# A decoder layer on one core: 46 products of the tile of ones ahead of TensorE's first real product

## The chip, the core and the metric

The kernel runs on one core of one Trainium2 chip. Its time is the device time of one launch in microseconds (us). A core has five engines, each with an instruction queue of its own that is worked through in order: TensorE (PE) for matrix products, VectorE (DVE), ScalarE (ACT), GpSimd (POOL) and SyncE (SP). SP issues all the DMA transfers of this kernel. An engine waits at an instruction until the semaphores that it needs have come, and everything behind that instruction on the same engine waits too.

## The reference

One layer of a decoder, in float32, for a prompt of 1024 tokens and 8 single-token samples that share the weights (1032 columns in all):

```python
z = x @ w_in                                   # 1024 -> 7680 columns, for all branches and gates
xr, yr, q, k, v, xq, g = jnp.split(z, SPLIT_IDX, axis=-1)
a_out = rg_lru(causal_conv(xr)) * gelu(yr)     # branch A: recurrence
s_out = sliding_window_attention(q, k, v)      # branch B: window 128, 16 heads
c_out = mem_attn(xq, mem_k, mem_v)             # branch C: 256 memory tokens, 4 heads
merged = sum(sigmoid(g_n + b_n) * (br_n @ w_branch[n]) for n in range(3))
h = layer_norm(ALPHA * x + merged @ w_out)
y = layer_norm(ALPHA * h + (silu(h @ w_gate) * (h @ w_up)) @ w_down)
```

The state of the recurrence, the last keys and values and the memory keys and values are outputs too.

## The kernel before, in words

Activations lie transposed: channels on the 128 partitions, the 1032 tokens along the free dimension. A float32 product is made of three products of the type `fp32r`: each operand is split into a high part (a cast on ACT, line L80) and a low part (a subtraction on DVE, L81), and high x high, high x low and low x high are added up in PSUM. So each tile that TensorE reads needs first a DMA, then a cast on ACT, then a subtraction on DVE.

The first stage, `project`, computes `x @ w_in` in 30 **units** of two row tiles each. Unit 0 (`begin`) is computed straight: four **quarters** of 258 columns, each with 48 products (2 halves of the channels, 2 row tiles, 4 blocks of 128 channels, 3 products each; lines L211 to L213, PSUM tile `u`, operands `th`/`tl` for x and `thw`/`tlw` for the weights). Its operands come from the first transfers: weights `ur<-win` and quarters of x, `x<-xQ`, both on SP's queue.

From unit 1 on a unit is computed with seven products of half the size in place of eight (Strassen's scheme, `fast_step`, lines L293 to L295): seven **steps** i = 0 to 6, each with 24 products of 128x258, first 12 for one half of the columns (p = 0) and then 12 for the other (p = 1). Step i needs the weights `u_ih` (ACT) and `u_il` (DVE); some of them are sums of blocks, `us`, made on DVE (L278). It needs also sums of quarters of x, made once for all units on DVE (L218, names `x`), and their casts and subtractions (`th`, `tl`). The results gather in PSUM tiles: `ub` takes the steps 0, 2, 4 and 6 one upon another, `ud` the steps 1 and 5, `uc` step 3. Between step 0 and step 2 ACT copies `ub` away (`p1s`, L318), and step 2 may not add to `ub` before that copy; in the same way `u2s` stands between the steps 2 and 4, and `zb<-ub` on DVE (L322) between the steps 4 and 6. PSUM has three `mm` buffers for `ub`, two `t` for `ud` and `u`, two `s` for `uc`, and one `o` for small things.

Beside the units run **side jobs** that other branches need. Two of them matter here. `dec_mem` (L791 on) is the memory attention of the eight samples for the first head: the query columns of unit 0 are transposed on TensorE (`drt`, L787), copied by ACT (`drow_c`, L788), written to DRAM (`dcq<-drow_c`, L789), read back broadcast to all partitions (`dcq<-dcq`, L800), and multiplied on DVE with the memory keys (`dcj`, L806). `lru` is the recurrence: DVE makes the convolution `xc` out of `za` of unit 1 (L728, L729), ACT and DVE split it (`xch`, `xcl`), and TensorE multiplies it with the gate blocks (`g`, L114 to L116, from `mm3`).

The order on each engine isn't written out by hand. The source hands all instructions to a scheduler at build time, with their dependences; it places them by priority and by times that it estimates for itself, engine by engine, and that order is then fixed in the program. `issue_after` ties a few groups behind a given instruction. An instruction that is added in one place can thus move others.

`self.ones` is a constant tile of 128x128 with 1/1024 in each element, set by DVE at the very start (L145) and used much later by the layer norms.

Of the kernel before, what the change touches and what calls it, by code (L numbers as in the profile page):

```python
# [18 lines left out]
P = 128  # L19
# [19 lines left out]
HT = T // 2  # L39
QN = T // 4  # L40
QS = 264
UNITS = (
    ("xq", 0), ("lru", 0), ("gate", 0), ("xq", 1), ("lru", 1), ("gate", 1), ("xq", 2), ("lru", 2), ("gate", 2),
    ("xq", 3), ("lru", 3), ("gate", 3), ("k", 0), ("lru", 4), ("v", 0), ("q", 0), ("lru", 5), ("gate", 4),
# [15 lines left out]
class Builder:  # L60
# [75 lines left out]
    def setup(self):  # L136
# [9 lines left out]
        self.shift = self.cst.tile([P, P], F32R, name="shift")  # L146
        nc.vector.memset(self.shift.bitcast(F32), -1.0 / (256 * MIX))

    def load_consts(self):
        nc, io = self.nc, self.io  # L150
        nc.sync.dma_start(self.vec, io["vec"])
        nc.sync.dma_start(self.ident, io["cst"][:, 0:P])
# [11 lines left out]
    def begin(self, rows, finish, load_next, next_quarter):  # L164


        nc, io, h = self.nc, self.io, D // 2
        place = lambda i: (self.tpe if i in (0, 1, 2, 3) else self.tpl, f"c{i}")

        def pair(name, i):  # L170
            pool, tag = place(i)
            return tuple(pool.tile([P, 4, QS], F32R, tag=tag, name=f"t{e}{name}", bufs=4) for e in "hl")

        x, hl, ts, w, ps = {}, {}, [[None] * 7, [None] * 7], [[None] * 2, [None] * 2], {}
        cols = lambda th, p: slice(HT * th + QN * p, HT * th + QN * (p + 1))

        def weight(j, e):
            raw = self.half_raw(io["win"][rows[j]][:, e * h:(e + 1) * h], h, f"ur0_{j}{e}")
            if e == 0:
                w[j] = [None, None, pair(f"w{j}", 4)]  # L180
            flat = [a.rearrange("p k n -> p (k n)")[:, e * h:(e + 1) * h] for a in w[j][2]]
            w[j][e] = flat
            return lambda: self.split(*flat, raw)

        def keep(name, i, src, sign=1.0):
            tiles = pair(name, i)
            hi, lo = (a[:, :, :QN] for a in tiles)
            src = src.rearrange("p (k n) -> p k n", k=4)
            if sign < 0:
                self.split_scaled(hi, lo, src, sign)  # L190
            else:
                self.split(hi, lo, src)
            return tiles

        def fetch(kh, th, p):
            x[kh, th, p] = self.x_quarter(kh, th, p)

        def block(kh, th, p):
            hl[kh, th, p] = keep(f"{kh}{th}{p}", {(0, 0): 0, (0, 1): 6, (1, 0): 3, (1, 1): 5}[kh, th], x[kh, th, p])

        def quarter(th, p, z):
            tags = ("mm", "t")
            for kh in range(2):
                xh, xl = (a[:, :, :QN] for a in hl[kh, th, p])
                for j in range(2):
                    if kh == 0:
                        ps[j] = self.bank(tags[j], f"u0{th}{p}{j}")[:, :QN]
                    wh, wl = w[j][kh]
                    for k in range(4):
                        c, first, last = slice(k * P, (k + 1) * P), kh + k == 0, kh == 1 and k == 3  # L210
                        nc.tensor.matmul(ps[j], wh[:, c], xh[:, k, :], start=first, stop=False)  # L211
                        nc.tensor.matmul(ps[j], wh[:, c], xl[:, k, :], start=False, stop=False)
                        self.last_mm = nc.tensor.matmul(ps[j], wl[:, c], xh[:, k, :], start=False, stop=last).ins  # L213
            for j in range(2):
                nc.scalar.copy(z[j][:, cols(th, p)], ps[j])

        def change(op, p, to, a, b):
            nc.vector.tensor_tensor(x[(*to, p)], x[(*a, p)], x[(*b, p)], op)  # L218
            return x[(*to, p)]

        s00 = weight(0, 0)
        fetch(0, 0, 0)
        s10, s01 = weight(1, 0), weight(0, 1)
        fetch(1, 0, 0)
        s11 = weight(1, 1)
        for th, p in ((0, 1), (1, 0), (1, 1)):
            fetch(0, th, p)
            fetch(1, th, p)
        z = self.zt("za0"), self.zt("zb0")
        s00()  # L230
        block(0, 0, 0)
        s10()
        s01()
        block(1, 0, 0)
        s11()
        quarter(0, 0, z)
        for th, p in ((0, 1), (1, 0), (1, 1)):
            block(0, th, p)
            block(1, th, p)
            quarter(th, p, z)  # L240
            if (th, p) == (1, 0):
                load_next()
                next_quarter(0)
        for p in range(2):
            ts[p][0], ts[p][3], ts[p][5] = hl[0, 0, p], hl[1, 0, p], hl[1, 1, p]
            change(ALU.subtract, p, (1, 1), (1, 1), (0, 1))
            ts[p][1] = keep(f"1_{p}", 1, change(ALU.subtract, p, (0, 1), (0, 0), (0, 1)))
        next_quarter(1)
        for p in range(2):
            ts[p][2] = keep(f"2_{p}", 2, change(ALU.add, p, (0, 0), (1, 1), (0, 0)), -1.0)  # L250
        next_quarter(2)
        next_quarter(3)
        for p in range(2):
            ts[p][4] = keep(f"4_{p}", 4, x[1, 1, p])
        for p in range(2):
            ts[p][6] = keep(f"6_{p}", 6, change(ALU.subtract, p, (1, 0), (0, 0), (1, 0)))
        views = lambda pair_: [tuple(a[:, k, :QN] for a in pair_) for k in range(4)]
        return [[views(t) for t in tp] for tp in ts], z
# [78 lines left out]
    def project(self):  # L337
# [7 lines left out]
        self.side, self.pumped = (deque(), deque()), 0  # L345
        n = len(UNITS)
        finish = [Finish(self, kind, j) for kind, j in UNITS]
        st = {}
# [1152 lines left out]
```

## Time and profile before

| | |
|---|---|
| time, median of 3 runs (range) | 1955.7 us (1953.8 to 1955.99) |
| the profiled execution | 1960.06 us, of which its span 1958.3 us |
| mean granted TensorE clock in the profile | 0.996 |
| busy share of the span: PE, DVE, ACT, POOL | 98%, 69%, 49%, 5% |
| products on PE | 14286 |
| bytes moved by DMA | 265.15 MB, mean 135 GB/s |

A row of the timeline gives the start and the length in us, the engine, the line, the operation with out<-in, the shape, how many, and in brackets the idle time before it with what ended it. Matmuls are pipelined: the length of one holds its latency, and the pace of TensorE is read from the distance between two starts. A row of the windows gives, for a stretch of time, its length and then for each engine busy us and (count), the granted TensorE clock (`PEclk`, 1.00 is full), the DMA share and GB/s. The list of waits gives who waited for whom, us in total, times, longest.

### The profile page before, as it was taken

The numbers are of one execution on the slowest core, as the hardware profiler recorded it, in microseconds if no ns is written. First come the engines' busy times: TensorE is split into PE (matmuls) and PEld (weight loads), VectorE is DVE, ScalarE is ACT, GpSimd is POOL, SyncE is SP. The second block draws the span as 40 slices with busy tenths as digits, with TensorE's granted clock in tenths as the row PEclk, the third lists the DMA queues.
The fourth block names the chain that finished last, engine by engine and source line by source line (L and its number), as shares of the span: only waits on it lengthen the run. The fifth ranks groups of instructions, "written<-read, shape, count | busy, mean of one in ns | idle before, by whom it ended". The sixth has DMA issues, their size and how long they took to land.

```text
span 1958.3 us, 37175 instructions
## 1 busy us (share of the span) xinstructions
PE 1920.2 (98%) x14286; PEld 1888.4 (96%) x14286; DVE 1345.4 (69%) x2871; ACT 960.8 (49%) x2093; POOL 99.8 (5%) x138
## 2 busy tenths in 40 slices
PE   8999999999999999999999999999999999999997
PEld 8999999999999999989999999999999999999996
DVE  8888788777766645389877457886666656734457
ACT  6556555556555545388765234644333333412214
POOL 0000012000000000011210000000000000000002
PEclk9999999999999999999999999999999999999999
DMA  5455544473233767567625242222333222523202
GB/s 212 159 189 165 181 160 164 151 239 112 84 136 124 258 221 223 152 170 213 165 71 181 88 149 77 90 66 82 114 104 98 103 87 76 185 74 124 84 1 88
DMA packets 154851, 265.15 MB, mean 135 GB/s; under 512 B 18624, under 2 KB 76816, under 8 KB 154640
## 3 DMA queue, kind: packets, MB, share of 16 engines
q1 hardware_dynamic: 154672, 262.76, 41.7%
q8 instruction: 112, 1.84, 0.4%
q14 instruction: 67, 0.55, 0.1%
HBM read 194.75 MB, written 70.03 MB: 135 GB/s over the span
## 4 chain that ended last, share of the span: by engine, by line
PE 84%; DVE 5%; ACT 5%; DMA 4%; issue 1%; SPq 0%; ACTq 0%; DVEq 0%; POOL 0%; POOLq 0%
PE ub L295 5%; PE ub L293 5%; PE ub L294 5%; PE fb L293 4%; PE fb L294 4%; PE fb L295 4%; PE d L115 3%; PE d L116 3%; PE d L114 3%; PE ud L295 2%; PE ud L294 2%; PE ud L293 2%; PE fd L293 2%; PE fd L295 2%; PE fd L294 2%; PE brs L115 2%
## 5 line engine op out<-in xcount | busy, mean ns | idle before, releaser
L582 ACT ACTIVATE bp<-bp,bst 128x257 f32<-128x257 f32 (+1 forms) x128 | 62.8, 493 | 17.6 <-DVE bst L578 17.4
L295 PE MATMUL ub<-th,u_0l 128*128 128x258 f32 x232 | 65.8, 284 | 2.1 <-DVE u_0l L81 2.1
L293 PE MATMUL ub<-th,u_0h 128*128 128x258 f32 x232 | 65.5, 282 | 1.4 <-ACT zb L1373 1.4
L1252 DVE SCALAR_TENSOR_TENSOR acc<-d,acc 128x388 f32<-128x388 f32 (+2 forms) x48 | 24.7, 514 | 61.0 <-PE d L116 61.0
L293 PE MATMUL ub<-th,u_6h 128*128 128x258 f32 x232 | 66.2, 285 | 0.3 <-DVE zb L322 0.2
L295 PE MATMUL ub<-th,u_4l 128*128 128x258 f32 x232 | 65.9, 285 | 0.3 <-DVE u_4l L81 0.3
L295 PE MATMUL ub<-th,u_2l 128*128 128x258 f32 x232 | 66.0, 285 | 0.0
L295 PE MATMUL uc<-th,u_3l 128*128 128x258 f32 x232 | 65.9, 284 | 0.0
L295 PE MATMUL ud<-th,u_1l 128*128 128x258 f32 x232 | 65.9, 284 | 0.0
L295 PE MATMUL ud<-th,u_5l 128*128 128x258 f32 x232 | 65.9, 284 | 0.0
L293 PE MATMUL uc<-th,u_3h 128*128 128x258 f32 x232 | 65.8, 283 | 0.0
L293 PE MATMUL ud<-th,u_5h 128*128 128x258 f32 x232 | 65.7, 283 | 0.0
L295 PE MATMUL ub<-th,u_6l 128*128 128x258 f32 x232 | 65.7, 283 | 0.0
L293 PE MATMUL ud<-th,u_1h 128*128 128x258 f32 x232 | 65.6, 283 | 0.0
L294 PE MATMUL ub<-tl,u_0h 128*128 128x258 f32 x232 | 65.6, 283 | 0.0
L293 PE MATMUL ub<-th,u_4h 128*128 128x258 f32 x232 | 65.6, 283 | 0.0
L293 PE MATMUL ub<-th,u_2h 128*128 128x258 f32 x232 | 65.6, 283 | 0.0
L294 PE MATMUL ub<-tl,u_2h 128*128 128x258 f32 x232 | 65.4, 282 | 0.0
L294 PE MATMUL ud<-tl,u_1h 128*128 128x258 f32 x232 | 65.4, 282 | 0.0
L294 PE MATMUL uc<-tl,u_3h 128*128 128x258 f32 x232 | 65.3, 282 | 0.0
L294 PE MATMUL ub<-tl,u_4h 128*128 128x258 f32 x232 | 65.3, 282 | 0.0
L294 PE MATMUL ud<-tl,u_5h 128*128 128x258 f32 x232 | 65.3, 282 | 0.0
(831 smaller groups left out, 8084.9 us busy)
## 6 DMA issues: line engine op xcount, KB each, us to landing
ur<-win SPq DMA_DIRECT2D x120, 256.0 KB, 2.9
urf<-wgu SPq DMA_DIRECT2D x80, 256.0 KB, 2.7
scr_f<-fo SPq DMA_DIRECT2D x36, 258.0 KB, 2.0
dck<-cmk SPq DMA_DIRECT2D x32, 256.0 KB, 3.2
dcv<-cmvT SPq DMA_DIRECT2D x32, 256.0 KB, 3.3
st<-scr_q SPq DMA_DIRECT2D x32, 256.0 KB, 4.3
S1L<-scr_f SPq DMA_DIRECT2D x14, 516.0 KB, 5.1
scr_g<-za SPq DMA_DIRECT2D x12, 516.0 KB
```

The source lines that it names most:

```text
L114: nc.tensor.matmul(ps, sh, mh, start=i == 0, stop=False)
L115: nc.tensor.matmul(ps, sh, ml, start=False, stop=False)
L116: self.last_mm = nc.tensor.matmul(ps, sl, mh, start=False, stop=closes and i == last).ins
L293: mm(sh[:, w], xh, start=opens and k == 0, stop=False)
L294: mm(sh[:, w], xl, start=False, stop=False)
L295: self.last_mm = mm(sl[:, w], xh, start=False, stop=k == 3).ins
L582: nc.scalar.activation(x, x, AF.Exp, bias=st[:, g:g + 1], scale=-1.0, accum_out=st[:, 4 + g:5 + g])
L1252: nc.vector.scalar_tensor_tensor(a, ps, MIX, a, op0=ALU.mult, op1=ALU.add)
```

## The change

A new function `keep_busy` issues 46 products of the tile of ones with itself, 128x128x128 each, into the one `o` buffer of PSUM. They add up in one accumulation group, and nobody reads the result. `begin` calls it right after the first weight and before the first quarter of x are loaded, so that they stand ahead of all other products in the source.

```diff
+WARM = 46
...
+    def keep_busy(self):
+        ps = self.bank("o", "warm")[:, :P]
+        for i in range(WARM):
+            self.nc.tensor.matmul(ps, self.ones, self.ones, start=i == 0, stop=i == WARM - 1)
...
         s00 = weight(0, 0)
+        self.keep_busy()
         fetch(0, 0, 0)
```

The lines behind these are 1 (from L42), 6 (from L150) and 7 (from L229) higher in the changed kernel; the text goes on using the numbers of the kernel before.

On TensorE the 46 products become the first instructions. They need only the memset of `ones`. Beside that the scheduler places instructions of the first 130 us or so in another order; behind that the order is the same on all engines. Three places matter. In the names `u1`, `u2` is the unit, and the last number only tells buffers apart (it is shifted by 47 in the change).

**DVE, end of unit 1.** Before, where the first low weights of unit 2 (`u2_0l`) are made:

```order
L386 SCALAR_TENSOR_TENSOR zb0_144<-zb0_144,hi_xq1_580 128x1024
L81 TENSOR_TENSOR u1_6l_602<-ur1_11_339,u1_6h_601 128x512
L806 SCALAR_TENSOR_TENSOR dcj0_0_0_597,dcs0_592<-dck0_0_595,dcq0_0_593 128x256
L320 TENSOR_TENSOR za1_605<-uc1_0_606,p1s1_0_478 128x258
L806 SCALAR_TENSOR_TENSOR dcj0_0_1_599,dcs0_592<-dck0_0_595,dcq0_0_593 128x256
L320 TENSOR_TENSOR za1_605<-uc1_1_620,p1s1_1_493 128x258
L81 TENSOR_TENSOR u2_0l_635<-ur2_00_495,u2_0h_634 128x512
```

And in the change, from the same subtraction on:

```order
L82 TENSOR_TENSOR u1_6l_649<-ur1_11_386,u1_6h_648 128x512
L327 TENSOR_TENSOR za1_652<-uc1_0_653,p1s1_0_525 128x258
L327 TENSOR_TENSOR za1_652<-uc1_1_667,p1s1_1_540 128x258
L82 TENSOR_TENSOR u2_0l_682<-ur2_00_542,u2_0h_681 128x512
L329 SCALAR_TENSOR_TENSOR zb1_685<-ub1_0_512,p5s1_0_569 128x258
...
L285 TENSOR_TENSOR us2_2_786<-us2_1_754,ur2_00_542 128x512
L813 SCALAR_TENSOR_TENSOR dcj0_0_0_644,dcs0_639<-dck0_0_642,dcq0_0_640 128x256
L689 RECIPROCAL lruc_712<-lruc_712 128x8
```

The first `dcj`, which needs the broadcast transfer `dcq`, stood four rows ahead of `u2_0l`; now it stands twelve rows behind it, after both `us` of unit 2. The rows left out are seven of the 128-partition constants of the recurrence, one `us` and one `zb`.

**TensorE, unit 2, steps 3 and 4, with the first gate product `g`.** Before:

```order
L295 MATMUL uc2_1_939<-th101_217,u2_3l_786 128x258
L114 MATMUL g0_0_0_953<-xch0_0_916,wgh0_910 128x344
L293 MATMUL ub2_0_789<-th4_0_443,u2_4h_831 128x258
...
L294 MATMUL ub2_0_789<-tl4_0_444,u2_4h_831 128x258
L115 MATMUL g0_0_0_953<-xcl0_0_917,wgh0_910 128x344
L116 MATMUL g0_0_0_953<-xch0_0_916,wgl0_911 128x344
L295 MATMUL ub2_0_789<-th4_0_443,u2_4l_832 128x258
```

In the change:

```order
L302 MATMUL uc2_1_986<-th101_264,u2_3l_833 128x258
L115 MATMUL g0_0_0_1000<-xch0_0_963,wgh0_957 128x344
L116 MATMUL g0_0_0_1000<-xcl0_0_964,wgh0_957 128x344
L117 MATMUL g0_0_0_1000<-xch0_0_963,wgl0_958 128x344
L300 MATMUL ub2_0_836<-th4_0_490,u2_4h_878 128x258
```

Eleven products of step 4 stood between the product with `xch` and the one with `xcl`; now the one with `xcl` comes at once, and all of step 4 stands behind it.

**ACT, unit 1, around the copies `p1s`.** Before:

```order
L80 CAST u1_2h_435<-us1_2_433 128x512
L80 CAST u1_3h_439<-ur1_01_335 128x512
L80 CAST th4_1_447<-x111_141 128x4x258
L318 COPY p1s1_0_478<-ub1_0_465 128x258
L318 COPY p1s1_1_493<-ub1_1_480 128x258
```

In the change:

```order
L392 ACTIVATE hi_xq0_621<-za0_190 128x1024
L81 CAST th4_1_494<-x111_188 128x4x258
L81 CAST th6_0_499<-x100_174 128x4x258
L325 COPY p1s1_0_525<-ub1_0_512 128x258
L325 COPY p1s1_1_540<-ub1_1_527 128x258
```

The cast `th6`, which needs a sum of quarters from DVE (`x100`), stood seven rows behind `p1s`; now it stands ahead of it. Further down on ACT the copy `drow_c`, which stood ahead of the casts of `u1_4h` and `u1_5h`, now stands behind both.

## The prediction

> **What bounds the kernel now.** I read the profile's page first, then the list of TensorE's waits, then the timeline where these waits lie. The page's first lines and its chain of waits:
>
> ```profile
> span 1958.3 us, 37175 instructions
> ...
> PE 84%; DVE 5%; ACT 5%; DMA 4%; issue 1%; SPq 0%; ACTq 0%; DVEq 0%; POOL 0%; POOLq 0%
> ```
>
> TensorE carries 84% of the chain that ended last. So a microsecond that TensorE loses or saves early comes through to the end, unless a later instruction waits for something else. The list of its waits over the span begins so:
>
> ```profile
> PE u L211 <- ACT th L80: 6.6, 1, 6.6
> PE ub L295 <- DVE u_0l L81: 2.1, 1, 2.1
> PE mv L446 <- ACT wmv_3h L80: 1.4, 2, 1.2
> ...
> PE ub L295 <- DVE u_4l L81: 0.3, 1, 0.3
> ```
>
> The longest is the start: 6.6 us until the first operands. The second and the fourth row belong to the end of unit 1, where the change moves instructions. Now the start in the timeline:
>
> ```profile
> 0.81 0.17 DVE L145 MEMSET ones<- 128x128 f32 x1 [0.81 <-PEq L1486]
> ...
> 6.60 1.23 DVE L81 TENSOR_TENSOR tl<-x,th 128x1032 fp32r<-128x1032 f32 x1 [1.76 <-ACT th L80]
> ...
> 7.89 0.58 PE L212 MATMUL u<-tl,thw 128*128 128x258 f32 x1 [0.17 <-DVE tl L81]
> ...
> 8.49 0.42 PE L211 MATMUL u<-th,thw 128*128 128x258 f32 x1
> ...
> 9.55 1.23 DVE L81 TENSOR_TENSOR tl<-x,th 128x1032 fp32r<-128x1032 f32 x1 [0.51 <-ACT th L80]
> ...
> 10.21 0.37 PE L213 MATMUL u<-th,tlw 128*128 128x258 f32 x1
> ...
> 10.89 0.28 PE L213 MATMUL u<-th,tlw 128*128 128x258 f32 x1
> ...
> 14.47 0.28 PE L213 MATMUL u<-th,tlw 128*128 128x258 f32 x1
> ```
>
> TensorE works without a break only from 7.89 on, when the first low part of x is there. From 8.49 to 10.21 eight products pass, 0.215 us each; from 10.89 to 14.47 thirty, 0.119 each. So TensorE starts at about half its pace and is let to the full one between 10.2 and 10.9. The row at 14.47 is the last of quarter 0.
>
> **Step 1: does the block of 46 fit into the wait?** It can start when `ones` is set, at about 1.0, and costs nothing if it is over by 7.87: 6.87/46 = 0.149 us a product. No row shows this product. The nearest:
>
> ```profile
> 710.15 1.91 PE L499 MATMUL cpt<-ident,cp 128*128 128x128 f32 x8
> 728.75 1.04 PE L499 MATMUL cpt<-ident,cp 128*128 128x128 f32 x8
> ...
> 839.83 0.23 PE L574 MATMUL bs<-ks,st 128*128 128x128 f32 x1
> 839.89 0.27 PE L575 MATMUL bs<-ks,st 128*128 128x128 f32 x1
> ```
>
> The transposes of 128x128 give the upper bound: less the latency of the last, (1.04 - 0.27)/7 = 0.11 at the full pace and (1.91 - 0.42)/7 = 0.21 at the half one. All 46 at 0.21 end at 10.8. The two `bs` products, fp32r tiles like `ones`, stand 0.06 apart, or 0.12 at half pace: all over by 6.5. I take the middle of the pair, 0.17 at half and 0.085 at full pace: with 3.6 us at half pace, as before from 6.6 to 10.2, 21 products pass, and the other 25 take 2.1 us. The block ends at about 6.7: cost nothing, hidden by the wait for x; bounds 0 and 10.8 - 7.9 = 2.9 us.
>
> [...]
>
> **Step 2: what the full pace is worth.** If the block lets the clock up, the twelve distances from 7.89 on that took 0.215 take 0.119: 12 x 0.096 = 1.15 us. The second half of quarter 0 now waits for its own low part, which is ready at 9.55 + 1.23 = 10.78 and would be asked for at about 10.7: -0.06. And one product that ran in the gap before 7.89 now stands behind it: -0.12. Quarter 1 starts 0.95 us earlier. Bounds: 0.95 and, with a block that ends at 10.8 but leaves full pace, 10.8 + 48 x 0.119 = 16.5 against 14.6, 1.9 late.
>
> [...]
>
> **Step 3: does it last to unit 1?** Rows for this and for the next steps:
>
> ```profile
> 16.16 2.38 DVE L81 TENSOR_TENSOR tl<-x,th 128x1032 fp32r<-128x1032 f32 x2 [0.87 <-ACT th L80]
> ...
> 20.98 0.69 DVE L81 TENSOR_TENSOR u_0l<-ur,u_0h 128x512 fp32r<-128x512 f32 x1 [1.30 <-ACT u_0h L80]
> ...
> 30.80 1.22 DVE L218 TENSOR_TENSOR x<-x,x 128x1032 f32<-128x1032 f32 x1
> 31.95 1.22 DVE L87 SCALAR_TENSOR_TENSOR tl<-x,th 128x1032 fp32r<-128x1032 f32 x1
> ...
> 36.58 0.68 DVE L81 TENSOR_TENSOR u_3l<-ur,u_3h 128x512 fp32r<-128x512 f32 x1
> 37.19 1.22 DVE L81 TENSOR_TENSOR tl<-x,th 128x1032 fp32r<-128x1032 f32 x1
> ...
> 47.59 0.68 DVE L81 TENSOR_TENSOR u_6l<-ur,u_6h 128x512 fp32r<-128x512 f32 x1
> ```
>
> A big DVE row costs 1.15 us (30.80 to 31.95), a weight row 0.61. Between 20.98 and 48.2, the end of `u_6l`, DVE has no gap. The change fills the gaps of 0.87 and 1.30 ahead of it (ACT's copies of `u` stand later, and one sum moves up), so I set DVE 2.2 us earlier: `u1_6l` ends at 46.0. Counting back over the twelve rows from behind `x100` to `u1_6l` (seven big ones, `x101` among them, and five weight rows): 7 x 1.15 + 5 x 0.61 = 11.1, so `x100` is ready at 34.9. Then ACT casts `th4` and `th6` (0.96 each) ahead of `p1s` (0.28): 37.1 to 37.2. Step 2, which needs that copy, would be reached at 37.57 - 0.95 = 36.6:
>
> ```profile
> 37.57 0.28 PE L293 MATMUL ub<-th,u_2h 128*128 128x258 f32 x1
> ...
> 43.56 0.28 PE L293 MATMUL ub<-th,u_4h 128*128 128x258 f32 x1
> ...
> 49.85 0.28 PE L293 MATMUL ub<-th,u_0h 128*128 128x258 f32 x1
> ```
>
> So 0.6 of the 0.95 is lost in a wait for `p1s`; some 0.3 is left.
>
> **Step 4: the wait at `u_0l`.** DVE stood at the first `dcj` until the broadcast `dcq` had landed, and `u_0l` was queued behind it:
>
> ```profile
> 50.24 0.42 DVE L806 SCALAR_TENSOR_TENSOR dcj<-dck,dcq 128x256 f32<-128x256 f32 x1 [1.98 <-DMA dcq<-dcq]
> ...
> 51.27 0.42 DVE L320 TENSOR_TENSOR za<-uc,p1s 128x258 f32<-128x258 f32 x1
> 51.61 0.68 DVE L81 TENSOR_TENSOR u_0l<-ur,u_0h 128x512 fp32r<-128x512 f32 x1
> ...
> 52.34 0.39 PE L295 MATMUL ub<-th,u_0l 128*128 128x258 f32 x1 [2.10 <-DVE u_0l L81]
> ```
>
> In the change only two `za` (0.34 each) stand between: `u_0l` is ready at 46.0 + 0.7 + 0.6 = 47.3. TensorE's steps 4 and 5 take 48 x 0.119 = 5.7 instead of 49.85 - 43.56 = 6.3, and end at about 49.0; step 6 needs nothing later than that (`zb<-ub`, 47.6), and `u_0` comes behind it. Saved: 0.3 + 0.6 + 2.3 (52.34 - 49.97, less one distance) = 3.2 us at the start of unit 2's step 1.
>
> **Step 5: what is late next.** The head of the line is only moved: behind `dcj` are now `u_1l`, `u_2l`, the convolution `xc` and `xcl`, and TensorE meets the product with `xcl` eleven products earlier in its order. The chain of waits has the two transfers:
>
> ```profile
> 42.23 2.83 DMA dcq<-drow_c
> 45.07 5.07 DMA dcq<-dcq
> ```
>
> And the timeline has what waited behind them:
>
> ```profile
> 67.76 0.51 DVE L81 TENSOR_TENSOR xcl<-xc,xch 128x344 fp32r<-128x344 f32 x1
> ...
> 68.33 0.43 PE L115 MATMUL g<-xcl,wgh 128*128 128x344 f32 x1
> ...
> 70.33 0.32 PE L114 MATMUL g<-xch,wgh 128*128 128x344 f32 x1
> ```
>
> `drow_c` now waits on ACT for `u1_5h`, thus for `us1_5` (46.0 - 2 x 1.15 - 2 x 0.61 = 42.5) and ends at 43.3; the two transfers take 2.83 and 5.07: `dcq` lands at 51.2, 1.0 later than before. From the first `dcj` to the end of `xcl` DVE took 68.27 - 50.24 = 18.0; fourteen rows of that now stand ahead (two `za`, two `zb` 0.34 each, `u_0l` and two `us` 0.61 each, seven constants below 0.1 each, together some 3.7). So `xcl` ends at 51.2 + 14.3 = 65.5. TensorE is there at 57.97 - 3.2 + 72 x 0.12 = 63.4, plus `g` with `xch`: 63.6, and waits 1.9 us. Two `g` of 0.16 and 24 products of step 4 later the next `g` starts at 65.6 + 0.3 + 2.9 = 68.8, where it was 70.33: **1.5 us saved**. (57.97 is the start of step 1 before: from 52.34, 47 products on.) Bounds: if `xcl` doesn't bind, 3.2; if `dcq` lands 3 us later, -1.5. Further on DVE and ACT have slack until 103, where their order is the old one; behind 130 us all orders are, and I carry 1.5 to the end.
>
> **Sum.** Clock 0.3, u_4l and u_0l 2.9, xcl -1.7: 1.5 us off the profiled execution, 1960.06 - 1.5 = 1958.6; that execution lies 4.4 above the median of the runs, so the median becomes 1955.7 - 1.5 = **1954.2 us**.
>
> **Rivals.** A difference below 0.2% (3.9 us) can't be told from none here; the runs alone spread over 2.2.
>
> *Nothing moves (the ones don't lift the clock, and the stall passes whole to `xcl`).* 1955.7, within 0.2%. For it: `xcl` is nearly as late. Against: `dcj` was 2 us of pure waiting. 15%.
>
> *The half clock in mid-kernel goes away.* The windows of the profile:
>
> ```profile
> 705.00:710.00 5.00, 3.46 (x27) 3.06 (x26) 1.72 (x3) 2.71 (x6) 0.00 (x0) 1.00 0.59 194
> 710.00:715.00 5.00, 5.00 (x25) 4.73 (x24) 2.83 (x5) 3.07 (x8) 0.00 (x0) 0.51 0.59 207
> ```
>
> After an idle 1.5 us in 705 to 710 the clock is at 0.51 for 5 us. [...] Against: this is one execution, and before had the same chance. 15%.
>
> *Slower: `dcq` lands late.* In the change SP has the stores of `za` and `zb` ahead of `dcq<-dcq`, and DVE waits at `dcj` with `u_1l` and `xcl` behind. It breaks even when `dcq` lands at 52.7; at 57 it costs 4.3, about 1960. For it: the transfer took 5.07 for little data. Against: the stores wait only for rows that end by 45.4, before `dcq` can be issued (46.1). 10%, of which 6 above 0.2%.
>
> *The forecast*, 0.5 to 3.2 us saved: 60%; its own range 1952.5 to 1955.2.
>
> **The numbers.** Faster by over 0.2%: the second rival, 15%, and little more: 0.16. Slower: 0.07. Within 0.2%: 0.77. The range adds the runs' spread and the clock stage to the bounds: 1950.2 to 1957.8.
>
> **What would show it.** Step 1: the first `th,thw` product not later than 7.9. Step 2: distances of 0.12 from the first product on. Step 3: a wait of about 0.6 for `p1s` near 37. Step 4: the row `ub <- u_0l` gone. Step 5: a new row `g <- xcl` of about 2 us near 65. Wrong is the forecast if the block ends behind 9, if DVE waits at `dcj` past 53, or if a wait stands where I found none, between 70 and 130.

## The result and the profile after

The change makes the kernel slower by 0.19%: 1958.88 us (median of 14 runs, 1954.86 to 1964.74) against 1955.48 us (14 runs of the kernel before beside them, 1952.46 to 1961.79), a ratio of 1.0019 with a 95% interval of 1.0011 to 1.0027. A second comparison gave 1.0017 (1.0007 to 1.0026). The forecast was 1954.2 us with a range up to 1957.8; the time lies 1.1 us above it. The profiled execution took 1958.62 us with a span of 1956.8, which is 1.4 us less than the profiled one before. So a difference of two single executions has here even the wrong sign; the places in the trace have to be compared.

The timeline of TensorE in the changed kernel, from the start:

```profile
1.03 10.08 PE L153 MATMUL warm<-ones 128*128 128x128 f32 x46 [1.03 <-DVE ones L146]
10.91 0.52 PE L217 MATMUL u<-th,thw 128*128 128x258 f32 x1
11.23 0.42 PE L218 MATMUL u<-tl,thw 128*128 128x258 f32 x1
...
14.02 0.39 PE L219 MATMUL u<-th,tlw 128*128 128x258 f32 x1
14.24 0.30 PE L217 MATMUL u<-th,thw 128*128 128x258 f32 x1
14.38 0.28 PE L218 MATMUL u<-tl,thw 128*128 128x258 f32 x1
14.50 0.28 PE L219 MATMUL u<-th,tlw 128*128 128x258 f32 x1
```

The 46 products take 10.91 - 1.03 = 9.88 us, 0.215 each, and the first real product starts at 10.91. The stream of quarter 0 starts at 11.23, where it was 7.89: 3.3 us late. And it starts at half pace: from 11.23 to 14.02 thirteen distances of 0.215 pass, and only from 14.38 on the distance is 0.12. The block of 46 has not let the clock up. The window view of the same kernel has to be read with care here (columns: us, busy us and count of PE, PEld, DVE, ACT and POOL, granted clock, DMA share, GB/s):

```profile
6.00:9.00 3.00, 3.00 (x16) 3.00 (x16) 2.40 (x3) 1.71 (x3) 0.00 (x0) 1.00 0.95 377
```

It shows a granted clock of 1.00 in the middle of the block. The clock records of the trace begin only with full clock, at 14.26 us here and at 10.38 in the kernel before, and hold nothing ahead of that. So at the start the pace has to be taken from the distances.

The waits of TensorE up to 130 us in the changed kernel are these two, and no others:

```profile
PE warm L153 <- DVE ones L146: 1.0, 1, 1.0
PE ub L300 <- ACT zb L1380: 0.8, 1, 0.8
```

The wait of 2.1 us for `u_0l` is gone, as forecast, and no wait for `p1s` or `xcl` has come in its place: TensorE is too late to wait for them. DVE still stands at the first `dcj`, where the broadcast transfer lands only now:

```profile
52.99 0.43 DVE L813 SCALAR_TENSOR_TENSOR dcj<-dck,dcq 128x256 f32<-128x256 f32 x1 [1.38 <-DMA dcq<-dcq]
```

Where TensorE stands behind all moved rows is read from the transposes into `dct` (some 670 rows into TensorE's order in all kernels here). The next four rows are from the view by tile: of the kernel before, of the change, of the order alone and of the block alone, which are two of the experiments below. They give durations in ns (least, median, most), then the first and the last start:

```profile
L812 PE MATMUL dct<-ident,dcs x2: 270/272/273, 92.9 to 93.0; 128*8 128x128 f32 x2
```
```profile
L819 PE MATMUL dct<-ident,dcs x2: 270/272/273, 93.4 to 93.6; 128*8 128x128 f32 x2
```
```profile
L818 PE MATMUL dct<-ident,dcs x2: 270/272/273, 91.5 to 91.6; 128*8 128x128 f32 x2
```
```profile
L825 PE MATMUL dct<-ident,dcs x2: 270/272/273, 94.9 to 95.0; 128*8 128x128 f32 x2
```

At this **mark** the change is 0.5 us behind. Of the 3.3 us lost at the start, the new order has won most back by then. The third row is the new order without the block, 1.4 us ahead of before; the fourth is the block without the new order, 2.0 us behind.

The mark is not the last place where TensorE waits in this stretch. The first step of a later unit waits near 122 until ACT has read an earlier `ub` out (`zb`, L1373). Before, in the list of waits and in the timeline:

```profile
PE ub L293 <- ACT zb L1373: 1.4, 1, 1.4
```
```profile
122.50 0.39 PE L293 MATMUL ub<-th,u_0h 128*128 128x258 f32 x1 [1.38 <-ACT zb L1373]
```

In the change:

```profile
122.04 0.39 PE L300 MATMUL ub<-th,u_0h 128*128 128x258 f32 x1 [0.82 <-ACT zb L1380]
```

Here ACT decides, and it is 0.5 us earlier in the change. So at 122 us the change is no longer behind the kernel before, and its second profile has this row at 122.08. Against the order alone, which has it at 121.11, 120.22 and 120.94 in its three profiles, the change is 0.9 to 1.9 us late. Its loss in the runs is larger than either.

In mid-kernel the half clock is there as before in this profile:

```profile
705.00:710.00 5.00, 2.10 (x9) 1.68 (x8) 1.72 (x3) 2.34 (x5) 0.00 (x0) 0.72 0.53 175
710.00:715.00 5.00, 5.00 (x29) 4.79 (x28) 2.36 (x4) 3.46 (x8) 0.00 (x0) 0.60 0.51 172
```

It follows a wait of TensorE that is longer than before (1.2 us there, and 2.8 here, the longest of the whole span):

```profile
PE mv L453 <- ACT wmv_3h L81: 2.8, 1, 2.8
```

### The profile page after: what moved, and what is told of

The parts are those of the page before. It is cut to its first block, busy times and chain, and to the rows that moved or that the text cites. A ratio compares the mean times of both kernels' runs of the same rounds, so it can differ in the third digit from the quotient of the medians.

```text
span 1956.8 us, 37273 instructions
## 1 busy us (share of the span) xinstructions
PE 1926.8 (98%) x14332; PEld 1897.0 (97%) x14332; DVE 1345.7 (69%) x2871; ACT 961.5 (49%) x2093; POOL 98.9 (5%) x138
## 4 chain that ended last, share of the span: by engine, by line
PE 88%; DMA 4%; ACT 4%; DVE 3%; issue 1%; SPq 0%; ACTq 0%; DVEq 0%
PE ub L302 5%; PE ub L301 5%; PE ub L300 5%; PE fb L300 4%; PE fb L301 4%; PE fb L302 4%; PE ud L302 3%; PE ud L301 3%; PE ud L300 3%; PE d L116 3%; PE d L117 3%; PE d L115 3%; PE fd L300 2%; PE fd L302 2%; PE fd L301 2%; PE op L116 2%
```

## The experiments

Theory A: the block costs, since it ends too late and leaves the clock at half. Theory B: the moved order costs. Theory C: neither does, and what was measured is how often the clock is halved in mid-kernel. To tell A from B, the order had to be held while the block changes. This was done with edges that only fix an instruction's place on its engine and make it wait for nothing: for each engine the rows between the first and the last that differ are chained in the wanted order (123 rows on DVE, 71 on ACT, 28 on SP, 473 on PE). In all kernels below that have "the change's order" or "the order before", every engine has exactly that order outside of the block. Line numbers are shifted by up to 8 against the change for that reason. The block's sum is read by nothing, so its length and its shape change no output.

The edit that they share, in the function that builds the program (`ORDER` holds, for each engine, places in the order in which the source traces its instructions, the block not counted; 46 stands for the number of products in the block, 0 in the order alone):

```diff
         Builder(ctx, tc, io).build()
+        traced = list(nc.cur_bb.bb.instructions)
+        warm = [i for i in traced if isinstance(i, mybir.InstMatmult)][:46]
+        traced = [i for i in traced if i not in warm]
+        for row in ORDER:
+            for a, b in zip(row, row[1:]):
+                tc.add_manual_dep(traced[b], traced[a].name, mybir.DependencyInfo(mybir.DependencyClass.NoSync, mybir.DependencyReason.DATA), reason="order")
```

What all timed runs gave, each beside runs of the kernel before on the same chip:

| kernel | block ends | mark | median us (runs) | before | ratio, 95% interval |
|---|---|---|---|---|---|
| the order alone | none | 91.5 | 1954.97 (11) | 1956.46 | 0.9991, 0.9983 to 1.0000 |
| the order alone, again | none | 91.1 | 1956.08 (12) | 1956.31 | 0.9996, 0.9985 to 1.0006 |
| 46 products, order before | 10.9 | 94.9 | 1959.54 (11) | 1956.46 | 1.0015, 1.0006 to 1.0023 |
| 16 products | 4.7 | 91.4 | 1954.96 (12) | 1956.81 | 0.9992, 0.9982 to 1.0002 |
| 16 products, again | 4.7 | 91.6 | 1954.54 (12) | 1957.21 | 0.9991, 0.9981 to 1.0002 |
| 23 products | 6.2 | 92.0 | 1954.65 (12) | 1957.21 | 0.9992, 0.9980 to 1.0003 |
| 27 products | 6.9 | 91.4 | 1956.00 (11) | 1955.78 | 1.0001, 0.9992 to 1.0010 |
| 30 products | 7.5 | 91.7 | 1958.34 (11) | 1956.46 | 1.0009, 1.0000 to 1.0018 |
| 30 products, again | 7.5 | 92.0 | 1959.68 (12) | 1956.31 | 1.0015, 1.0004 to 1.0026 |
| 36 products | 8.8 | 91.0 | 1955.01 (11) | 1955.78 | 0.9985, 0.9975 to 0.9996 |
| the change, again (46) | 10.9 | 93.6 | 1958.71 (12) | 1956.31 | 1.0017, 1.0007 to 1.0026 |
| 92 products | 20.7 | 102.5 | 1966.85 (6) | 1956.46 | 1.0049, 1.0036 to 1.0062 |
| 16 products of 512 columns | 7.4 | 91.9 | 1955.45 (12) | 1956.31 | 0.9993, 0.9983 to 1.0003 |
| the same, again | 7.2 | 91.7 | 1955.63 (12) | 1957.21 | 0.9990, 0.9979 to 1.0001 |
| 30 products of 512 columns | 10.4 | 91.7 | 1956.32 (12) | 1957.21 | 0.9995, 0.9985 to 1.0004 |

Where nothing else is said, the order is the change's. The block's end is the start of the first real product, or for 16 and 23 products the end of the block's row; the mark is the first row of `dct` in the one profile. The ratio is worked out from all runs and need not be that of the two medians (for 36 products that would be 0.9996). The runs were made on five chips. The order alone, the blocks of 30, 46 and 92 and the first of the two rows of 16 wide products ran on two of them, all other rows on the other three.

### The order without the block

```diff
-        self.keep_busy()
```

> The change's order of instructions on every engine, without the block of 46 (the block's result is read by nothing, so no output changes). Theory A, the block itself is what costs: TensorE starts as before (first product 6.6, stream from 7.9, twelve distances at 0.215 and then 0.119), the wait of 2.1 us for u_0l is gone, and the time is 0 to 2 us below the kernel before, about 1954, so 4 to 5 us below the change. Theory B, the moved order costs: the time stays with the change, about 3.5 us above before, although the start is the old one. Theory C, neither: what was measured is how often the clock is halved in mid-kernel; then this run also scatters between 1955 and 1964, and its clock, not its start, goes with the time.

> The change's order without the block, a second time, beside the change itself and the block of 30, on one chip. Its first 11 runs had a median 1.5 us below before and a granted clock of 0.998 in most of them, where before had 0.996 to 0.998. If the order is what saves, it is again 1 to 2 us below before and 4 to 5 us below the change. If the first result was the luck of the clock, it is within 1 us of before.

> A third profile of the order without the block, as the partner of the looks at the block of 30: the wait for wmv_3h 0.3 to 0.5 us and no half-clock stage between 700 and 800, if these belong to the kernel; a wait of over 1.2 us or a stage, if they come by chance.

Its waits up to 130 us:

```profile
PE u L217 <- ACT th L86: 6.4, 1, 6.4
PE ub L299 <- ACT zb L1379: 1.4, 1, 1.4
PE u L218 <- DVE tl L87: 0.7, 1, 0.7
PE g L121 <- DVE xcl L87: 0.5, 1, 0.5
```

The time is 1.5 and 0.2 us below before (23 runs together: 1955.43, where 137 runs of before have 1956.59). Theory B falls: the moved order costs nothing. At the mark it saves 1.3 to 1.8 us in its three profiles; in the runs the saving is about 1 us, and with intervals that reach 1.0000 and 1.0006 it is hardly set apart from none. The steps on the order hold: the wait at `u_0l` is gone, and a new one stands at `g <- xcl`, at 65.48. The single execution took 1958.0 us, with a wait for `wmv_3h` of 1.2 us and a half-clock stage at 705 to 715; the other two profiles had waits of 0.4 and 0.3 us and no stage there. So the stage comes by chance also without a block.

### The block without the order, and twice the block

```diff
-WARM = 46
+WARM = 92
```

> The block of 46 in front, but every engine's other instructions in the order of the kernel before. Theory A: the block ends at 10.9 again, and quarter 0 is some 3.5 us late; the wait of 2.1 us for u_0l at 52 hides a part of this, since the transfer that it waits for does not hang on TensorE's first products, so the time is 1.3 to 3.5 us above before. Theory B (the order costs): the time is that of before, within 1 us. If this and the order alone add up to the change, the two act apart; if the block alone costs more than the change, the order had in truth saved something.

> The change with twice the block, 92 products of the tile of ones, the other instructions in the change's order. Theory A: 46 more products at 0.215 us end at about 20.8 instead of 10.9, and 9.9 us more stand in the time: about 1968.8. If products of 128 columns can lift the clock at all, it rises inside the block (at 14.2 by the change's trace): then 31 products take 0.11 and the block ends at about 17.6, with the real products at 0.119 from the first; the time is then about 1965. Theory B or C: the start is hidden by later waits, and the time stays within 2 us of the change.

> The change itself a second time, as the partner of the other three on the same chip: 3 to 4 us above before if the first comparison holds; 3 us above the block of 30 if what costs is that the block ends at 10.9 instead of 7.5.

The block alone costs 3.1 us. Of the wait at `u_0l` (2.1 before) 0.7 is left, so it hides 1.4 us of the late start, as theory A has it. At the wait for `zb` near 122 the block alone is 1.0 us behind before (123.48); the other 2 us arise later:

```profile
PE warm L159 <- DVE ones L152: 1.0, 1, 1.0
PE ub L306 <- ACT zb L1386: 0.8, 1, 0.8
PE ub L308 <- DVE u_0l L88: 0.7, 1, 0.7
PE ub L308 <- DVE u_4l L88: 0.3, 1, 0.3
```

The block of 92 costs 10.4 us against before and stands 9.6 us behind it at the mark, 8.5 at the wait for `zb`. In the runs it lies 8 us above the change (1958.88 and 1958.71), where the expectation had 9.9. Its products by tile, and the rows behind them:

```profile
L159 PEld LDWEIGHTS warm<-ones x92: 288/333/338, 1.0 to 20.4; 128*128 128x128 f32 x92
L159 PE MATMUL warm<-ones x92: 415/415/472, 1.0 to 20.5; 128*128 128x128 f32 x92
```
```profile
20.72 0.52 PE L223 MATMUL u<-th,thw 128*128 128x258 f32 x1
...
22.33 0.42 PE L224 MATMUL u<-tl,thw 128*128 128x258 f32 x1
22.55 0.37 PE L225 MATMUL u<-th,tlw 128*128 128x258 f32 x1
22.76 0.28 PE L223 MATMUL u<-th,thw 128*128 128x258 f32 x1
22.88 0.28 PE L224 MATMUL u<-tl,thw 128*128 128x258 f32 x1
```

For 19.7 us TensorE makes one product of 128 columns after the other, each in 0.214 us, and the pace stays at half. Behind them 2.04 us of real products with 258 columns pass (20.72 to 22.76) until the distance is 0.12. A block of this kind does not lift the clock, at 46 products (9.88 us) and at 92 (19.7 us). So twice the time in such products does not do it; the next experiment changes the kind of product.

### Products with more columns

```diff
-        ps = self.bank("o", "warm")[:, :P]
+        ps = self.bank("o", "warm")[:, :512]
+        wide = self.wpool.tile([P, D // 2], F32R, tag="qh", name="wide", bufs=5)[:, :512]
+        self.nc.gpsimd.memset(wide.bitcast(F32), 1.0 / D)
-            self.nc.tensor.matmul(ps, self.ones, self.ones, start=i == 0, stop=i == WARM - 1)
+            self.nc.tensor.matmul(ps, self.ones, wide, start=i == 0, stop=i == WARM - 1)
```

> The block as 16 products of the tile of ones with a tile of 512 columns of ones (a memset on GpSimd makes it), the other instructions in the change's order. At half pace a product of 512 columns should take 0.43 us (258 columns take 0.215), so the block ends at 8.0 at the latest, and earlier if the clock rises inside it. If products with many columns lift the clock where the ones with 128 did not, the real products stand 0.12 apart from the first one on (at about 7.9), and quarter 0 is over 1 to 2 us earlier than in the order alone; by the steps behind it 0 to 1 us of that is left at 92 us, and the time is 1953.5 to 1956, level with or just below the order alone. If the clock does not rise either, the distances are 0.215 until 10 to 14 us, and the time is that of the block of 30.

> The 16 products with 512 columns, a second time. The first time it was 0.9 us below before, with full pace from the first real product on. If the full pace at the start were worth its 1 us, it would be below the order alone and the block of 16 of the same chip by as much; by the trace the head start is gone at 92 us (91.9 against 91.1 to 91.5), and then the three are level.

> 30 products with 512 columns instead of 16, in the change's order: 6.3 us for the first 16 and 0.215 us for each of the other 14 at full pace end at 10.4 to 10.8, as late as the change's block, but with the clock up. Lateness alone: quarter 0's 48 products take 0.12 from the first one on, end at 16.2 instead of 17 in the change, and the time is 2 to 3 us above the order alone. If the clock was all that cost, the time is that of the order alone or less, 1955; if the clock played no part, it is the change's, 1958.7.

Here the clock rises. With 16 products:

```profile
1.29 6.30 PE L161 MATMUL warm<-wide,ones 128*128 128x512 f32 x16 [1.29 <-POOL wide L159]
7.43 0.28 PE L225 MATMUL u<-th,thw 128*128 128x258 f32 x1
7.54 0.28 PE L226 MATMUL u<-tl,thw 128*128 128x258 f32 x1
7.67 0.28 PE L227 MATMUL u<-th,tlw 128*128 128x258 f32 x1
...
37.95 0.39 PE L308 MATMUL ub<-th,u_2h 128*128 128x258 f32 x1 [0.80 <-ACT p1s L333]
```

From the first real product on the distance is 0.12; inside the block it falls from 0.43 to 0.23 us some 4.5 to 5 us after the first product (the 16 take 7.43 - 1.29 = 6.14 us, where 0.43 each would be 6.9). And the head start goes as step 3 of the prediction said: at step 2 of unit 1, near 37, TensorE waits 0.8 us for `p1s`. At the mark the kernel is level with the order alone (91.9 and 91.7, against 91.1 to 91.5), and so is the time, within what the intervals can tell. No gain from warming the clock up is seen here, even where it works.

With 30 such products:

```profile
1.29 9.26 PE L161 MATMUL warm<-wide,ones 128*128 128x512 f32 x30 [1.29 <-POOL wide L159]
10.39 0.28 PE L225 MATMUL u<-th,thw 128*128 128x258 f32 x1
10.51 0.28 PE L226 MATMUL u<-tl,thw 128*128 128x258 f32 x1
```

They end 0.5 us before the change's block, but with the clock up. The mark is at 91.7, 1.8 us ahead of the change, and the time 1956.32, 0.9 us below before. So an end at 10.4 is caught up by 92 us, if full pace begins there; what the change loses at the mark, it loses by the half pace from 11.2 to 14.2 on top of the late end. Neither the lateness alone nor the half pace alone does it: the order alone has half pace up to 12.0 to 12.6 in its three profiles, but its stream starts at 7.1 to 7.7.

### Shorter blocks of 128 columns

```diff
-WARM = 46
+WARM = 16
```

and in the same way 23, 27, 30 and 36.

> 16 products of the tile of ones, 128 columns, the other instructions in the change's order. The block ends at 4.5, well before the first real product (6 to 7), and between the two TensorE is idle. Theory A2: any block of such products puts something off later in the kernel, whatever its end; then the median is again 3 us above the order alone (about 1959). Theory A3: what costs is that the block runs up to the first real product without having lifted the clock, or holds it past 7; then 16 products cost nothing and the median is that of the order alone, 1955 to 1956.

> The block of 16 in the change's order, a second time: 1 to 2 us below before, as the first time and as the order alone, if a block that ends in time is free; 3 us above that if the first result was chance.

> 23 products of the tile of ones, 128 columns, in the change's order. The block ends at 6.0, about when the first operand is there (5.9 to 6.6). If a block costs only once it holds up a real product, the median is that of the order alone, 1955 to 1956 (1 us below before). If the cost grows with the number of products from 16 on, it lies halfway, about 1957 to 1958.

> 27 products of the tile of ones, 128 columns, in the change's order; the block ends at 6.8, behind the arrival of the first operand (5.9 to 6.6) and ahead of the first low part (7.1 to 7.9). If the step lies where the block meets the first real product and TensorE no longer idles between them, the median is 2 to 3 us above before, as with 30; if it lies where it puts off the product with the low part, it is 2 us below before, as with 23; anything between says that the cost grows gradually.

> The change with 30 products of the tile of ones instead of 46, the other instructions in the change's order. At 0.215 us each the block ends at 7.5, before the first low part of x is there (7.9). Theory A: no delay at the start, and the time is that of the order alone, about 1954; if the block has TensorE's clock up earlier than 10.3, up to 1 us less. Theory B: the time of the change, 3.5 us above before. If the block of 30 puts the half pace off to 14 us as the block of 46 did, though it ends in time, then such products hold the clock down, and some 2 us of the loss remain.

> The block of 30 in the change's order, a second time. In its first profile the block ended in time, TensorE was level with the order alone at 92 us (91.7 against 91.5), and yet its median lay 3.4 us above the order alone. If a block costs only by ending late, the second median is within 1.5 us of the order alone. If something later in the kernel goes worse with any block, it is again 3 us above it, and the granted clock is again 0.997 or lower in all runs.

> One more execution of the block of 30 under the profiler. Both profiles so far have quarter 0 no later than the order alone, though 23 runs have a median 3.7 us above it. If the start is what costs in the usual run, this profile shows full pace only at 13 to 15 us and TensorE at the second half of unit 1 (first row of dct) at 93 or later instead of 91.7; if it is later, the loss shows between 690 and 850 as a longer wait for wmv_3h and a half-clock stage.

> As the look before it: a fourth profile of the block of 30. Waits for wmv_3h in the kernels with a block were 0.8 to 2.8 us, in those without 0.3 to 1.2; if the block makes this wait, it is over 1.2 again.

> 36 products, which end at 8.8, about 1 us late. If the cost is a step between 23 and 30, this lies with 30 and 46, at 2 to 3 us above before; if it follows the end of the block, halfway between 23 (2 below) and 46 (2 above): level with before; and if 30 is an accident of its own, it lies on that line too, below 30.

16 and 23 products show no cost: they lie 1.8 to 2.7 us below before, as the order alone or a little better. 27 lie 0.2 us above before, between 23 and 30, so these runs show no clear step there. 30 products cost as much as 46, twice: on the one chip that timed both they lie 3.4 and 2.4 us above before, and the order alone 0.2 below. Yet the block of 30 ends at 7.5, and all four profiles of that kernel have the mark at 91.6 to 92.0. And 36, which end later, show no cost: 0.8 us below before, a ratio of 0.9985. So the cost does not follow the end of the block. That 30 is an accident of its own is not shown, though: 30 and 36 were never timed on the same chip, so the chip, or the chance of the runs, may part them as well as the block. In the four profiles of the block of 30 full pace began at 12.2, 9.7, 12.3 and 11.9 us, no later than in the order alone (12.0 to 12.6). The two single executions of it took 1954.97 us, with a wait of 1.4 us for `wmv_3h` and no half-clock stage, and 1958.52 us, with a wait of 2.0 and a stage at 700 to 710. At the wait for `zb` its four profiles stand at 120.16 to 120.55, level with the order alone or ahead of it: its loss arises behind 122 us.

### What happens behind the mark

Twenty profiles, of all these kernels, were laid beside each other, with two stretches: from the mark to the first `bra` product (near 650) and from there to the first `bs` product (near 830). In the first stretch the four without a block take 558.2 to 560.5 us; fifteen of the sixteen with one, of whatever length, take 555.6 to 557.1 (the sixteenth, a run of the change, has a wait of 3.3 us for `xcl` at 225 and a half-clock window behind it). In the second stretch the four take 172.8 to 178.4 and the sixteen 174.6 to 183.1. TensorE comes earlier to the memory branch and waits longer there for `wmv_3h`: 0.3 to 1.2 us without a block, 0.4 to 2.8 with one. This is that wait in the order alone, and the clock behind it:

```profile
PE mv L452 <- ACT wmv_3h L86: 0.4, 1, 0.4
```
```profile
705.00:710.00 5.00, 4.24 (x35) 3.80 (x34) 2.74 (x5) 3.90 (x9) 0.00 (x0) 1.00 0.61 191
710.00:715.00 5.00, 5.00 (x36) 4.59 (x35) 2.50 (x4) 2.42 (x6) 0.38 (x2) 1.00 0.56 181
```

The profile with the most half clock is that of the block of 23 (1960.5 us, though the median of that kernel is 1954.65):

```profile
705.00:710.00 5.00, 4.66 (x28) 4.48 (x27) 2.62 (x5) 3.41 (x9) 0.00 (x0) 0.67 0.71 233
710.00:715.00 5.00, 5.00 (x25) 4.55 (x25) 1.12 (x2) 1.28 (x4) 0.38 (x2) 0.65 0.28 85
...
725.00:730.00 5.00, 5.00 (x21) 4.90 (x21) 0.56 (x1) 0.27 (x1) 0.00 (x0) 0.50 0.47 165
```

A window is 3.41 us at half clock in the clock records of these profiles (two in a row are 6.83, as from 710.1 on in the kernel before and from 707.2 on in the change), so 1.7 us of clock, 0.0009 of the span of 1958. Eight profiles without one between 655 and 825 take 175.5 us for the second stretch in the mean, seven with one 177.8, four with two 180.5, and this one, with four, 181.8. The granted clock of an execution goes with them: over the 137 executions of the kernel before beside these experiments the median time is 1955.0 us where the clock is 0.998 (45 of them), 1956.7 at 0.997 (60), 1959.25 at 0.996 (19) and 1960.3 at 0.995 (12). A straight line through the clock takes away 58% of the variance of the kernel before, but 24% of that of the block of 30 and 13% of that of 36: it is much of the spread, not all.

Nor is it most of the change's loss. With each 0.001 below 0.998 counted as one window, before has 1.0 of them in the mean, the change 1.2 (26 executions), the order alone 0.6 (23) and the block of 30 1.1 (23). At 2 us a window that is 0.4 of the change's 2.4 to 3.4 us. At the same clock the change lies 1.0 (at 0.998), 1.9 (at 0.997) and 2.2 us (at 0.996) above before. Theory C explains much of the spread and a small part of the difference.

A third stretch, from the first `bs` product to the start of TensorE's last, holds no half clock. There the four without a block take 1114.0 to 1115.3 us and the sixteen with one 1114.2 to 1117.1; a part of it is a wait for `bph` between 830 and 925, 0.6 to 0.7 us without a block and up to 2.5 with one. The four profiles of the block of 30 take 1116.7, 1116.0, 1114.5 and 1116.6, those of 16, 23, 27 and 36 take 1114.3 to 1115.3. This is the one stretch that sets the block of 30 apart, by some 1 us. But the two largest of the others are blocks of 512 columns (1117.1 and 1116.3), which show no loss in the runs, so it is a trace to follow and no explanation.

**What stays open.** That the block costs, and not the order, is shown by the runs with one order: the change lies 2.6 us above the order alone on the chip that timed both, the block of 30 lies 3.4 and 3.6 above it on two chips. Where it costs is shown in part. At the wait for `zb` the change is 0.9 to 1.9 us behind the order alone, and the block of 512 columns that ends nearly as late but at full pace is not; this part goes back to the late start and the half pace. The rest arises later, where the order is the same. Against the kernel before it is 0.4 to 0.5 us ahead at that wait, and the runs end 2.4 to 3.4 us behind (the kernel before has one profile, so this may be off by a microsecond). The block of 30 has lost nothing at that wait and ends 1.9 to 3.4 us behind before. What in the program decides was not found. Two things differ with the block and were not tried apart: it takes the one `o` buffer of PSUM first (what that moves is not shown, and it would be the same for 30 and 36), and it makes TensorE's program longer.

## Why the prediction was wrong, and where it was right

**Step 1 failed: the size of the product.** I took 0.17 us at half pace, "the middle of the pair", between two `bs` products that start 0.06 apart and the transposes with 0.21. It measured 0.215, the bound that I named; the block ends at 10.9, the bound being 10.8. The lower bound should never have stood in the sum. Each product of the block loads its own weights (46 loads in the trace, 0.213 to 0.214 us apart from the second on), and in the trace of before the loads around those two `bs` products never start closer than 0.11 us, at full clock:

```profile
839.83 0.19 PEld L575 LDWEIGHTS bs<-ks,st 128*128 128x128 f32 x1
839.95 0.19 PEld L574 LDWEIGHTS bs<-ks,st 128*128 128x128 f32 x1
840.06 0.19 PEld L575 LDWEIGHTS bs<-ks,st 128*128 128x128 f32 x1
840.18 0.19 PEld L116 LDWEIGHTS bra<-S0H,wba_l 128*128 128x128 f32 x1
```

The two products could stand 0.06 apart once, since the load of the first, the row ahead of these, had begun 0.17 us earlier, under longer products. A stream of loads does not come that fast: of the 14255 distances between two loads of 128 columns in this trace, 14 are below 0.10 us. The rows above stand 0.11 to 0.12 apart at full clock (1.00 from 838 to 842), and the block's 0.215 is twice that.

**Step 2 failed: the block does not lift the clock.** The "3.6 us at half pace, as before" was taken for a matter of time. With 128 columns it is not: 46 and even 92 products (9.88 and 19.7 us) stay at half pace to the end. The gain itself also hung on one execution: full pace begins at 10.4 in the profile of before and at 12.0 to 12.6 in the three of the order alone. (The "twelve distances" are eleven in the trace, 7.89 to 10.41, the first of 0.38; the sum stays at about 1.2 us.) In step 1 I took the pace of the product from two rows that looked like it, and did not ask what sets that pace; in step 2 I took any product for one that lifts the clock. Even my bad case, "a block that ends at 10.8 but leaves full pace", was too kind: quarter 1 starts at 18.2 (14.38 and 32 distances of 0.12), not at 16.5.

**The step to the end failed too.** The prediction says "behind 130 us all orders are, and I carry 1.5 to the end". The orders are the same there, but the times are not: where the forecast was 1.5 us faster, the change is 0.4 to 0.5 us faster at 122 us and 2.4 to 3.4 slower in the runs. Steps 1 and 2 account for the first difference, some 1 us. The rest is a term that the prediction put at nothing, a cost that the block has behind 122 us. Against the one profile of before it is 3 to 4 us, against the order alone on the same chip some 1 to 2, and its cause stays open. The block of 30 shows that step 1 alone would not have saved the forecast: it ends in time and costs as much.

**Step 3 was not reached in the change, and was right in kind.** TensorE came too late to wait for `p1s`. Where the clock is up at the start (512 columns), the wait is there at 37.95, with 0.8 us for the 0.6 of the sum.

**Steps 4 and 5 were right in kind, for the order alone.** The wait at `u_0l` is gone in all kernels with the change's order. The new wait at `xcl` stands at 65.48 instead of near 65, with 0.5 us instead of 1.9: both TensorE's gain ahead of it and its loss there were taken too large. That the net of 1.5 us came out (1.4 at the mark in that profile, 1.2 in the medians of all runs) is two errors that cancel, which is luck. `dcq` landed at 51.15 in the order alone, where the forecast had 51.2, and at 53.0 in the change, just past the 52.7 at which the rival "slower: `dcq` lands late" breaks even. In the change this costs nothing, as TensorE is late itself.

**The rivals.** "Nothing moves" had the right first half (the ones don't lift the clock) and no late start. "The half clock in mid-kernel goes away" is not borne out: the stage is at 705 to 715 in the first profile of the change and missing in the second, and by the granted clock the runs of the change have no fewer such windows (1.2) than before (1.0). The low end of the range, 1950.2, counts on this stage too; that a move of TensorE's products by 1.5 us takes it away no run shows: in the moved order alone it is there in one profile of three. The slower case that came true was not among the rivals: the late block stood in the text as the bound of step 1, a cost of 2.9 us, but I gave it no case and no chance of its own, and closed the range at 1957.8. That this bound lies near the loss of 2.4 to 3.4 us is luck, since a good part of that loss arises later. The sentence "wrong is the forecast if the block ends behind 9" names what happened at the start.

## What to carry to other kernels

When each product of a filler on TensorE loads its own weights, read its price from the load engine's rows in a stretch where loads follow each other, not from the distance of two products: here the loads stood 0.11 to 0.12 us apart at full clock and the block's products 0.215 at half pace, where two products had stood 0.06 apart. No filler made this kernel faster than its new order alone: 16 of 128 columns showed no cost, 30 and 46 cost 1.9 to 3.4 us, and 16 of 512 columns lifted the clock, but by 92 us the head start was gone, the next stage waiting for `p1s` and `xcl`. Do not stop at the start when you price a filler: the block of 30 fits into the wait and costs all the same, for a reason that was not found. And when a change also reorders the program, hold the order and take the added work out before blaming either.

## What the runs showed of the hardware

A product of 128x128 with 128 columns in `fp32r`, with its own weight load, takes 0.215 us at half pace (9.88 us for 46), as long as one with 258 columns (0.215, from 11.23 to 14.02 in the change). 92 of them in a row, over 19.7 us, left the pace at half; products with 512 columns had it up some 4.5 to 5 us after the first of them (their distance falls from 0.43 to 0.23 us).

The head of the kernel swallows a late start well: real products that begin at 10.4 at full pace stand at 92 us where those stand that begin at 7.7 at half pace (91.7 against 91.1 to 91.5).

Windows of half clock in the middle of the kernel come in two of three executions of the kernel before (92 of 137 have a clock below 0.998), and each goes with about 2 us more (medians of 1955.0, 1956.7, 1959.25 and 1960.3 us at clocks of 0.998 to 0.995). They come with a wait of TensorE: of the twenty profiles, the six whose wait for `wmv_3h` near 705 was at most 1.1 us had none between 655 and 825, and of the fourteen with a longer wait twelve had one or more.
